# An RG-LRU block on both channel halves at once, and its steps run beside the RWKV's in the last third

## The chip, the cores and the metric

The kernel runs on one NeuronCore of a Trainium2 chip. The metric is the device time of one execution in microseconds (us). A core has five engines, each with its own instruction queue that is worked off in order: PE (TensorE, the matmuls), DVE (VectorE), ACT (ScalarE, activation functions), POOL (GpSimd) and SP (SyncE, which here issues DMAs). They wait for one another by semaphores. ACT evaluates functions from tables; an ACT_TABLE_LOAD row is the load of another set of functions.

## The reference, cut to what matters

One layer of a hybrid streaming encoder on 2048 tokens (with 16 learned tokens ahead, T = 2064) of width 1024, in fp32. One input projection feeds three head groups; their outputs go through one output projection, and a gated FFN with a short convolution follows.

```python
p  = rms_norm(h, norm_mix_pre) @ w_in                  # 1024 -> 512 | 1544 | 1024 columns
xa, ya = split(p[..., :512]);  pb = p[..., 512:2056];  pc = p[..., 2056:]
oa = rg_lru_group(xa, ya, ...)                         # 256 channels: the change is here
ob = forgetting_attention_group(pb, ...)               # 8 heads of 64, causal
oc = rwkv7_group(pc, ...)                              # 4 heads of 64, a recurrence over tokens
h  = h + rms_norm(concat([oa, ob, oc]) @ w_out, norm_mix_post)
...                                                    # FFN: up, conv of 3, gelu(g) * v, down

def rg_lru_group(xa, ya, ...):
    u = causal_dwconv(xa, conv_w) + conv_b             # 4 taps
    r = sigmoid(u @ ga_w + ga_b);  i = sigmoid(u @ gx_w + gx_b)      # per head of 64
    log_a = -8 * r * softplus(-lam);  a = exp(log_a)
    b = sqrt(-expm1(2 * log_a)) * (i * u)
    h_t = a_t * h_{t-1} + b_t                          # scan over tokens
    return h * gelu(ya)
```

## The kernel before, in words

Every large fp32 matmul is made of three passes over operands that are split into a high and a low half (`mm3`, L174 to L176). The stages follow one another: the input projection in three parts of the tokens (784, 768 and 512 columns), attention, the output projection, the FFN's up projection and its down projection. In each part of the input projection 24 units of output columns are computed (`psp` tiles on PE); ACT and DVE empty PSUM (`stp`, `sth`, `stl`), and the rows go to DRAM (`scr_p`). Between parts the next tokens are normalised, transposed and split (`w_in_norm`, tiles `xh`, `xl`).

Beside the projection run the two recurrences. `Beside.advance` is called once per unit of the projection and steps a queue of Python generators at a pace of 1.25 steps a call; a part's generator, `recurrences`, is added after 14 units. What is left at the projection's end is issued by `beside.finish()`, ahead of attention. The generator takes blocks of 256 tokens, nine in all, three per part: (0, 1, 2), (3, 4, 5), (6, 7, 8). The first block has 208 tokens and the last 64. For each block it steps the RWKV's preparation and its triangular solve (`R.block`, up to the mark `SOLVED`), then the ending of the RWKV block before (`R.ending`), and then the RG-LRU block (`lru_block`, L1432 to L1490).

The RG-LRU block works on 128 channels at a time, so everything in it is done twice, for the halves p = 0 and 1. For each half: the raw rows come by DMA into `rwlraw`; the convolution is one activation (L1455) and three instructions on DVE (L1457); two matmuls give the gates (L1462, L1463, into the one PSUM buffer `eps`); activations and DVE instructions form a and b, among them the root (L1478); the scan is one DVE instruction (L1480); the second raw tile and a tanh form gelu(y) (L1484 to L1488); the product (L1489) goes to DRAM by one DMA (`scr_mix`). The root needs another table than Exp and Tanh, so an ACT_TABLE_LOAD stands before the root (L1478), and another before whichever activation of the other set comes next (L1487, L1077, L1078, or attention's L698). `rwlraw` and the result tile `rwlu` have two buffers, the other tiles one.

The order on each engine isn't written by hand: a scheduler arranges the program's instructions by a simulated timeline, and the program's order is one input to it. Each engine then works its queue in the order found. The attention (`Attn.run`, L823) starts behind the last projection unit in program order, and its first matmuls (`mx`, `sc`, `po`) share the engines with the RWKV's last blocks. `mc` is its maximum on DVE (L571), `p` its exponential on ACT (L698), `q` its query tiles, whose extra rows are filled by memsets (L469, L487 to L489).

Of the kernel before, what the change touches and what calls it, by code (L numbers as in the profile page):

```python
# [1 line left out]

# [981 lines left out]
class Rwkv:  # L984
# [127 lines left out]
    def chunks(self, b, nch, sg, rav, bk, wc, bon):  # L1112
# [321 lines left out]
def lru_block(core, R, scr, k, b):  # L1434

    nc = core.nc
    t0 = max(0, Rwkv.start(b))
    n = min(T, Rwkv.start(b + 1)) - t0
    c0 = PAD + t0
    tt = nc.vector.tensor_tensor  # L1440
    stt = nc.vector.scalar_tensor_tensor

    def tl(s):
        return R.t([P, 256], s, bufs=2 if s == "lu" else 1)[:, :n]

    def raw(row, a):
        t = R.t([P, 260], "lraw", bufs=2)[:, : c0 + n - a]
        nc.sync.dma_start(t, scr["p"][row : row + P, a : c0 + n])
        return t

    for p in range(2):
        pc = slice(p, p + 1)
        x = raw(P * p, c0 - 3)
        u, r, g, al = (tl("l" + s) for s in ("u", "r", "g", "a"))
        nc.scalar.activation(u, x[:, 3:], AF.Identity, scale=k["conv_w"][:, 6 + p : 7 + p], bias=k["conv_b"][:, pc])  # L1455
        for i in range(3):
            stt(u, x[:, i : n + i], k["conv_w"][:, 2 * i + p : 2 * i + p + 1], u, op0=ALU.mult, op1=ALU.add)  # L1457


        ps = R.pe()  # L1460
        pa, px = ps[:, :n], ps[:, 256 : 256 + n]
        nc.tensor.matmul(pa, k["ga_w"][:, p], u, start=True, stop=True)  # L1462
        nc.tensor.matmul(px, k["gx_w"][:, p], u, start=True, stop=True)  # L1463
        nc.scalar.activation(r, pa, AF.Abs, bias=k["ga_b"][:, pc])
        nc.vector.tensor_scalar(al, pa, k["ga_b"][:, pc], 0.0, op0=ALU.add, op1=ALU.min)
        nc.scalar.activation(g, px, AF.Tanh, scale=0.5, bias=k["rate"][:, 2, pc])
        nc.scalar.activation(r, r, AF.Tanh, scale=0.5)
        nc.scalar.activation(al, al, AF.Exp)
        stt(r, r, 1.0, al, op0=ALU.add, op1=ALU.mult)
        stt(g, g, 1.0, u, op0=ALU.add, op1=ALU.mult)  # L1470
        yield
        nc.scalar.activation(al, r, AF.Exp, scale=k["rate"][:, 0, pc])
        nc.scalar.activation(r, r, AF.Tanh, scale=k["rate"][:, 1, pc])

        tt(u, al, al, op=ALU.mult)
        stt(r, u, 1.0, r, op0=ALU.add, op1=ALU.mult)
        nc.vector.tensor_scalar(r, r, 1e-34, None, op0=ALU.max)
        nc.scalar.activation(r, r, AF.Sqrt)  # L1478
        stt(g, g, 0.5, r, op0=ALU.mult, op1=ALU.mult)
        nc.vector.tensor_tensor_scan(u, al, g, k["h"][:, pc], op0=ALU.mult, op1=ALU.add)  # L1480
        nc.vector.tensor_copy(k["h"][:, pc], u[:, n - 1 : n])

        ya, y = raw(2 * P + P * p, c0), r
        nc.scalar.activation(y, ya, AF.Square)  # L1484
        nc.vector.tensor_scalar(y, y, 0.044715, 1.0, op0=ALU.mult, op1=ALU.add)
        tt(y, y, ya, op=ALU.mult)
        nc.scalar.activation(y, y, AF.Tanh, scale=0.7978845608028654)  # L1487
        stt(y, y, 1.0, ya, op0=ALU.add, op1=ALU.mult)  # L1488
        stt(u, u, 0.5, y, op0=ALU.mult, op1=ALU.mult)  # L1489
        nc.sync.dma_start(scr["mix"][P * p : P * p + P, t0 : t0 + n], u)  # L1490
        yield

# [599 lines left out]
def recurrences(core, R, lk, f_bias, scr, blocks, part):  # L2092
# [14 lines left out]
_INS = [  # L2107
# [294 lines left out]
```

## Time and profile before

| what | value |
|---|---|
| time, three runs | 2982.83, 2985.45, 2989.7 us (median 2985.45) |
| profiled execution | 2982.66 us, span 2981.0 us, mean granted PE clock 0.974 |
| PE busy | 2855.9 us, 96% of the span |
| DVE busy | 2024.3 us, 68% |
| ACT busy | 1504.8 us, 50% |
| POOL busy | 1308.5 us, 44% |
| DMA | 530.51 MB, mean 178 GB/s |

The page has the busy time of each engine, the busy share in 40 slices, the chain of work that ended last (followed back from the end, at each step to what released it), and groups of instructions by source line. "L1478" is line 1478 of the kernel before; after the change the same code stands one to five lines lower. A group's row reads: line, engine, operation, output<-inputs, shapes, xcount | busy us, mean ns of one | idle us of the engine just ahead of them, and who ended that idle time. In the windows view a row is a stretch of the span. By the trace the first part of the projection runs with recurrences from about 150 us, the crossing to the second part lies at 285 to 325, the second part and its crossing up to about 640, the third part until about 855, and the RWKV's last blocks beside attention until about 1065 or a little later. Attention lasts to about 1500 us.

### The profile page before, as it was taken

The numbers are of one execution on the slowest core, as the hardware profiler recorded it, in microseconds if no ns is written. First come the engines' busy times: TensorE is split into PE (matmuls) and PEld (weight loads), VectorE is DVE, ScalarE is ACT, GpSimd is POOL, SyncE is SP. The second block draws the span as 40 slices with busy tenths as digits, with TensorE's granted clock in tenths as the row PEclk, the third lists the DMA queues.
The fourth block names the chain that finished last, engine by engine and source line by source line (L and its number), as shares of the span: only waits on it lengthen the run. The fifth ranks groups of instructions, "written<-read, shape, count | busy, mean of one in ns | idle before, by whom it ended". The sixth has DMA issues, their size and how long they took to land.

```text
span 2981.0 us, 53287 instructions
## 1 busy us (share of the span) xinstructions
PE 2855.9 (96%) x18826; PEld 2447.1 (82%) x18826; DVE 2024.3 (68%) x3957; ACT 1504.8 (50%) x2937; POOL 1308.5 (44%) x1569
## 2 busy tenths in 40 slices
PE   6999999999988889999999999999999999999998
PEld 6998899888875554566568999999999999787887
DVE  5257754665687766665546988798778777656766
ACT  4246432454346554455634666656565665324333
POOL 1001121132124566566842666455655444646443
PEclk8999899999988899999999999999999999999999
DMA  6776479576653348445245665576767764436453
GB/s 217 234 233 220 143 251 322 179 242 219 219 131 78 85 118 225 105 104 125 66 125 190 200 192 173 171 225 210 211 208 216 220 196 134 156 114 222 145 174 120
DMA packets 470343, 530.51 MB, mean 178 GB/s; under 512 B 86862, under 2 KB 356888, under 8 KB 468524
## 3 DMA queue, kind: packets, MB, share of 16 engines
q1 hardware_dynamic: 469308, 526.18, 58.4%
q8 instruction: 148, 2.42, 0.3%
q0 software_dynamic: 768, 0.93, 0.1%
q14 instruction: 119, 0.97, 0.1%
HBM read 368.07 MB, written 158.90 MB: 177 GB/s over the span
## 4 chain that ended last, share of the span: by engine, by line
PE 73%; DVE 8%; DMA 7%; ACT 4%; POOL 4%; issue 2%; SPq 1%; DVEq 0%; POOLq 0%; ACTq 0%
PE psu L174 9%; PE psu L175 9%; PE psu L176 9%; PE psp L176 4%; PE psp L174 4%; PE psp L175 4%; PE psd L174 4%; PE psd L175 4%; PE psd L176 4%; PE po L716 3%; PE pswo L174 2%; PE pswo L175 2%; PE pswo L176 2%; PE mx L566 2%; PE sc L693 2%
## 5 line engine op out<-in xcount | busy, mean ns | idle before, releaser
L175 PE MATMUL psu<-xo,uw 128*128 128x344 f32 x1848 | 592.4, 321 | 0.0
L174 PE MATMUL psu<-xo,uw 128*128 128x344 f32 x1848 | 587.0, 322 | 3.1 <-DVE vb L1870 2.8
L176 PE MATMUL psu<-xo,uw 128*128 128x344 f32 x1848 | 582.6, 320 | 0.6 <-DVE uw L1679 0.6
L174 PE MATMUL psp<-xh,wh 128*128 128x384 f32 (+2 forms) x1152 | 378.3, 328 | 1.4 <-DMA wh<-scr_wk 1.4
L176 PE MATMUL psp<-xh,wl 128*128 128x384 f32 (+2 forms) x1152 | 376.3, 327 | 0.5 <-DMA wl<-scr_wk 0.5
L175 PE MATMUL psp<-xl,wh 128*128 128x384 f32 (+2 forms) x1152 | 375.0, 326 | 0.0
L1679 DVE TENSOR_TENSOR uw<-uq,uw 128x512 fp32r<-128x512 f32 x341 | 316.0, 931 | 63.7 <-ACT uw L1678 60.3
L174 PEld LDWEIGHTS psu<-xo,uw 128*128 128x128 f32 x1848 | 346.4, 188 | 4.2 <-DVE vb L1870 3.6
L175 PEld LDWEIGHTS psu<-xo,uw 128*128 128x128 f32 x1848 | 347.8, 188 | 0.0
L176 PEld LDWEIGHTS psu<-xo,uw 128*128 128x128 f32 x1848 | 346.4, 188 | 1.4 <-DVE uw L1679 1.4
L1678 ACT ACTIVATE uw<-uq 128x512 fp32r<-128x512 f32 x462 | 287.8, 627 | 103.6 <-PE psu L176 52.9
L698 ACT ACTIVATE p<-sc,bias 128x512 f32<-128x512 f32 (+4 forms) x352 | 197.5, 590 | 156.3 <-PE sc L694 126.1
L571 DVE TENSOR_REDUCE mc<-mx 128x1 f32<-128x512 f32 (+5 forms) x352 | 190.7, 566 | 117.5 <-PE mx L566 83.0
L1818 DVE SCALAR_TENSOR_TENSOR uy<-psu,ffn_cols,uy 128x342 f32<-128x342 f32 (+1 forms) x390 | 220.7, 567 | 60.9 <-ACT uy L1816 59.1
L737 POOL TENSOR_TENSOR acc<-acc,p 128x512 f32<-128x512 f32 (+3 forms) x208 | 222.3, 1072 | 62.4 <-DVE acc L737 28.3
L1826 POOL TENSOR_TENSOR uy<-uy,uy 128x342 f32<-128x342 f32 (+1 forms) x132 | 147.1, 1115 | 228.7 <-DVE uy L1818 59.5
L1679 POOL TENSOR_TENSOR uw<-uq,uw 128x512 fp32r<-128x512 f32 x121 | 185.4, 1532 | 134.1 <-ACT uw L1678 115.3
L176 PEld LDWEIGHTS psp<-xh,wl 128*128 128x128 f32 x1152 | 218.0, 189 | 8.4 <-issue 5.8
L174 PEld LDWEIGHTS psp<-xh,wh 128*128 128x128 f32 x1152 | 217.8, 189 | 8.4 <-issue 4.5
L175 PEld LDWEIGHTS psp<-xl,wh 128*128 128x128 f32 x1152 | 217.8, 189 | 7.2 <-issue 5.7
L1679 DVE TENSOR_TENSOR fo<-u,fo 128x896 fp32r<-128x896 f32 x88 | 101.1, 1149 | 132.3 <-ACT fo L1678 130.4
L1678 ACT ACTIVATE fo<-u 128x896 fp32r<-128x896 f32 x88 | 81.2, 923 | 209.0 <-PE psd L176 108.1
(489 smaller groups left out, 6326.2 us busy)
## 6 DMA issues: line engine op xcount, KB each, us to landing
uq<-scr_us SPq DMA_DIRECT2D x220, 256.0 KB
uq<-in_ffn_up_dram SPq DMA_DIRECT2D x209, 256.0 KB
wl<-scr_wk SPq DMA_DIRECT2D x48, 512.0 KB
wh<-scr_wk SPq DMA_DIRECT2D x48, 512.0 KB
u<-scr_ff SPq DMA_DIRECT2D x88, 256.0 KB
scr_ff<-uy SPq DMA_DIRECT2D x110, 171.0 KB
raw<-in_w_in_dram SPq DMA_DIRECT2D x24, 512.0 KB
scr_wk<-wh SPq DMA_DIRECT2D x24, 512.0 KB
```

The lines of the kernel that those rows point to most:

```text
L174: nc.tensor.matmul(out, ah, bh, start=first, stop=False, skip_group_check=more)
L175: nc.tensor.matmul(out, ah, bl, start=False, stop=False, skip_group_check=more)
L176: nc.tensor.matmul(out, al, bh, start=False, stop=last, skip_group_check=more)
L566: nc.tensor.matmul(ps[:rows, : e - a], q3[:, qo : qo + rows], k2[:, a:e], start=True, stop=not last)
L571: self.reduced = nc.vector.tensor_reduce(mc[:rows, i, ci : ci + 1], ps[:rows, : e - a], axis=AX.X, op=ALU.max)
L698: last = nc.scalar.activation(p[:rows, :w], ps[:rows, :w], AF.Exp, bias=bias[:rows, j : j + 1])
L716: mm = nc.tensor.matmul(po[at : at + 64, c0:n], v1[:rows, j], p[:rows, : n - c0], start=start and i < 2, stop=end and i + 2 >= len(group), ...
L737: eng.tensor_tensor(a, ps_[0][0][:rows, c0:n] if start and i == 1 else a, p[:rows, : n - c0], op=ALU.add)
L1678: core.nc.scalar.activation(hi, src, AF.Copy)
L1679: (eng or core.nc.vector).tensor_tensor(lo, src, hi, op=ALU.subtract)
L1818: core.conved = stt(y[:, :n], src[:, i : n + i], cw[:, 44 * i + cc : 44 * i + cc + 1], y[:, :n], op0=ALU.mult, op1=ALU.add)
L1826: core.pooled = nc.gpsimd.tensor_tensor(v[:, :n], g[:, :n], v[:, :n], op=ALU.mult)
```

## The change

`lru_block` works on both halves at once: its tiles are [128, 2, 256], with one buffer each (before, two for `lu` and `lraw`). One DMA fetches the raw rows of both halves, one stores the result. The convolution, the matmuls, the activations with a bias or scale per channel and the scan are still issued per half; ten DVE instructions and five activations are issued once for both halves. So there is one root a block. The block is cut into four steps of the generator, as before, but elsewhere.

In the projection's last third the RG-LRU steps of blocks 6, 7 and 8 are chained into one generator, `early`, which is advanced by one step with every step of the RWKV's solve and of its ending; before, each of these blocks came behind the whole solve and ending of its number. In the first two thirds the place of the block stays. A scratch tile of the RWKV's last block is 12 instead of 16 wide.

```diff
+from itertools import chain
...
-        og = w3 if nch == 4 else self.t([P, 16, P], "xu")
+        og = w3 if nch == 4 else self.t([P, 12, P], "xu")
...
     def tl(s):
-        return R.t([P, 256], s, bufs=2 if s == "lu" else 1)[:, :n]
+        return R.t([P, 2, 256], s)[:, :, :n]
 
     def raw(row, a):
-        t = R.t([P, 260], "lraw", bufs=2)[:, : c0 + n - a]
-        nc.sync.dma_start(t, scr["p"][row : row + P, a : c0 + n])
+        t = R.t([P, 2, 260], "lraw")[:, :, : c0 + n - a]
+        nc.sync.dma_start(t, scr["p"][row : row + 2 * P, a : c0 + n].rearrange("(p r) t -> r p t", p=2))
         return t
...
+    act = nc.scalar.activation
+    x = raw(0, c0 - 3)
+    u, r, g, al = (tl("l" + s) for s in ("u", "r", "g", "a"))
     for p in range(2):
...
+        act(u[:, p], x[:, p, 3:], AF.Identity, scale=k["conv_w"][:, 6 + p : 7 + p], bias=k["conv_b"][:, pc])
...
+        act(r[:, p], pa, AF.Abs, bias=k["ga_b"][:, pc])
+        nc.vector.tensor_scalar(al[:, p], pa, k["ga_b"][:, pc], 0.0, op0=ALU.add, op1=ALU.min)
+        act(g[:, p], px, AF.Tanh, scale=0.5, bias=k["rate"][:, 2, pc])
+    yield
+    act(r, r, AF.Tanh, scale=0.5)
+    act(al, al, AF.Exp)
+    stt(r, r, 1.0, al, op0=ALU.add, op1=ALU.mult)
+    stt(g, g, 1.0, u, op0=ALU.add, op1=ALU.mult)
+    for p in range(2):
+        pc = slice(p, p + 1)
+        act(al[:, p], r[:, p], AF.Exp, scale=k["rate"][:, 0, pc])
+        act(r[:, p], r[:, p], AF.Tanh, scale=k["rate"][:, 1, pc])
+    yield
+    tt(u, al, al, op=ALU.mult)
+    stt(r, u, 1.0, r, op0=ALU.add, op1=ALU.mult)
+    nc.vector.tensor_scalar(r, r, 1e-34, None, op0=ALU.max)
+    act(r, r, AF.Sqrt)
+    stt(g, g, 0.5, r, op0=ALU.mult, op1=ALU.mult)
+    for p in range(2):
+        pc = slice(p, p + 1)
+        nc.vector.tensor_tensor_scan(u[:, p], al[:, p], g[:, p], k["h"][:, pc], op0=ALU.mult, op1=ALU.add)
+        nc.vector.tensor_copy(k["h"][:, pc], u[:, p, n - 1 : n])
+    yield
+    ya, y = raw(2 * P, c0), r
+    act(y, ya, AF.Square)
...
+    stt(u, u, 0.5, y, op0=ALU.mult, op1=ALU.mult)
+    nc.sync.dma_start(scr["mix"][0 : 2 * P, t0 : t0 + n].rearrange("(p r) t -> r p t", p=2), u)
+    yield
...
-    for b in ((0, 1, 2), (3, 4, 5), (6, 7, 8))[part]:
+    bs = ((0, 1, 2), (3, 4, 5), (6, 7, 8))[part]
+    early = chain.from_iterable(lru_block(core, R, scr, lk, b) for b in bs if part == 2)
+    for b in bs:
         gen = R.block(b)
         while next(gen) != R.SOLVED:
+            next(early, None)
             yield
-        yield from R.ending
+        for _ in R.ending:
+            next(early, None)
+            yield
         R.ending = gen
-        yield from lru_block(core, R, scr, lk, b)
+        if part < 2:
+            yield from lru_block(core, R, scr, lk, b)
```

What the scheduler makes of it is seen in the order of each engine. On PE, before, the gates of one half of block 7 (`eps` tiles, written from `rwlu`) stand among attention's first maxima and scores:

```order
L693 MATMUL sc_11586<-q_1444_11397,k_1424_11324 128x512
L694 MATMUL sc_11586<-q_1433_11344,k_1425_11325 128x512
L579 MATMUL mx_11512<-ident,sh_11510 1x128 x2
L1135 MATMUL rps_9956<-rwrav_9902,rwbk_9909 64x128 x8
L1462 MATMUL eps_10537<-rwlu_10529,lru_ga_w 128x256
L1463 MATMUL eps_10537<-rwlu_10529,lru_gx_w 128x256
L579 MATMUL mx_11512<-ident,sh_11510 1x128 x2
L566 MATMUL mx_11537<-k_1425_11325,q_1427_11329 128x400
```

Now the last gates of the kernel, those of block 8's second half, stand within the projection's last unit:

```order
L175 MATMUL psp_10291<-xh_6593,wh_10112 128x256
L176 MATMUL psp_10291<-xl_6594,wh_10112 128x256
L1463 MATMUL eps_9220<-rwlu_9202,lru_ga_w 128x64
L1464 MATMUL eps_9220<-rwlu_9202,lru_gx_w 128x64
L177 MATMUL psp_10291<-xh_6593,wl_10113 128x256
L175 MATMUL psp_10291<-xh_6593,wh_10112 128x256
```

So all RG-LRU matmuls moved ahead of the projection's end. Of the 3456 matmul rows of the projection, the gates of blocks 6, 7 and 8 now stand behind 3058, 3277 and 3413 of them; before, block 6 stood behind 3265 and the other two behind the last.

On ACT, at the crossing from the projection's first part to its second, these pieces stood before (`xh` is the split of the next tokens, `rww`, `rwsc`, `rwe` are the RWKV's):

```order
L1478 ACT_TABLE_LOAD
L1478 ACTIVATE rwlr_2971<-rwlr_2971 128x256
...
L1487 ACT_TABLE_LOAD
L1487 ACTIVATE rwlr_2971<-rwlr_2971 128x256
...
L1478 ACT_TABLE_LOAD
L1478 ACTIVATE rwlr_3071<-rwlr_3071 128x256
L1261 ACTIVATE rww_202_1647<-rps_2642 64x8x64 x2
L1078 ACT_TABLE_LOAD
L1078 ACTIVATE rwe_3379<-rwe_3379 128x512
```

And now:

```order
L152 ACTIVATE xh_3091<-pst_3224 128x4x128
L1481 ACT_TABLE_LOAD
L1481 ACTIVATE rwlr_2947<-rwlr_2947 128x512
L152 ACTIVATE xh_3091<-pst_3231 128x4x128
L1083 ACTIVATE rwsq_3343<-rwe_3331,rwkv_om 128x256
L1489 ACTIVATE rwlr_2947<-rwlraw_3080 128x512
L1253 ACTIVATE rwxf_2363<-rps_2599 32x8x32 x2
L1492 ACT_TABLE_LOAD
L1492 ACTIVATE rwlr_2947<-rwlr_2947 128x512
```

Two roots of 256 columns with a table load before and behind each became one root of 512 with one pair of loads. Over the kernel, ACT_TABLE_LOAD rows fall from 54 to 36.

On DVE, before, the RWKV's last reciprocal root (rows of 4x256) stood ahead of the projection's last `stl`:

```order
L77 SCALAR_TENSOR_TENSOR rwitmp_9834<-rwix_9833 4x256
L78 TENSOR_TENSOR rwitmp_9834<-rwitmp_9834,rwia_9832 4x256
L1273 COPY rwxu_9339<-rps_9352 128x256
L79 SCALAR_TENSOR_TENSOR rwix_9833<-rwitmp_9834,rwix_9833 4x256
L241 SCALAR_TENSOR_TENSOR stl_10299<-psp_10273,sth_10298 128x256
```

Now it stands among and behind attention's memsets and its first maxima:

```order
L1494 SCALAR_TENSOR_TENSOR rwlu_9202<-rwlu_9202,rwlr_9203 128x2x64
L490 MEMSET q_1378_11124 1x512
L76 TENSOR_SCALAR rwix_9664<-rwia_9663 4x256
...
L572 TENSOR_REDUCE mc_11150<-mx_11152 128x1
L78 SCALAR_TENSOR_TENSOR rwitmp_9665<-rwix_9664 4x256
L572 TENSOR_REDUCE mc_11150<-mx_11156 128x1
L1106 SCALAR_TENSOR_TENSOR rwsq_9657<-rwsq_9657,rwkv_cols,rwr_9724 128x256 x2
```

So the last of the RG-LRU has taken the place of RWKV work there: 21 RWKV rows of DVE that stood ahead of attention's first memset now stand behind it, and 56 of the RG-LRU's 58 rows behind it moved ahead of it. POOL's order and the count of PE's instructions stay the same; SP issues 27 DMAs fewer.

More of the change, by code (lines that the diff above doesn't have):

```diff
@@ L1451, in lru_block @@
+    x = raw(0, c0 - 3)
+    u, r, g, al = (tl("l" + s) for s in ("u", "r", "g", "a"))
     for p in range(2):
         pc = slice(p, p + 1)
-        x = raw(P * p, c0 - 3)
-        u, r, g, al = (tl("l" + s) for s in ("u", "r", "g", "a"))
-        nc.scalar.activation(u, x[:, 3:], AF.Identity, scale=k["conv_w"][:, 6 + p : 7 + p], bias=k["conv_b"][:, pc])
+        act(u[:, p], x[:, p, 3:], AF.Identity, scale=k["conv_w"][:, 6 + p : 7 + p], bias=k["conv_b"][:, pc])
         for i in range(3):
-            stt(u, x[:, i : n + i], k["conv_w"][:, 2 * i + p : 2 * i + p + 1], u, op0=ALU.mult, op1=ALU.add)
+            w = k["conv_w"][:, 2 * i + p : 2 * i + p + 1]
+            stt(u[:, p], x[:, p, i : n + i], w, u[:, p], op0=ALU.mult, op1=ALU.add)
@@ L1460, in lru_block @@
         ps = R.pe()
         pa, px = ps[:, :n], ps[:, 256 : 256 + n]
[L1462 to L1488, printed above, removed]
@@ L1489, in lru_block @@
-        stt(u, u, 0.5, y, op0=ALU.mult, op1=ALU.mult)
-        nc.sync.dma_start(scr["mix"][P * p : P * p + P, t0 : t0 + n], u)
-        yield
+        nc.tensor.matmul(pa, k["ga_w"][:, p], u[:, p], start=True, stop=True)
+        nc.tensor.matmul(px, k["gx_w"][:, p], u[:, p], start=True, stop=True)
+        act(r[:, p], pa, AF.Abs, bias=k["ga_b"][:, pc])
+        nc.vector.tensor_scalar(al[:, p], pa, k["ga_b"][:, pc], 0.0, op0=ALU.add, op1=ALU.min)
+        act(g[:, p], px, AF.Tanh, scale=0.5, bias=k["rate"][:, 2, pc])
```

4 lines of the change are left out of this document (added).

## The prediction

> **What bounds the kernel now.** I started with the page's chain that ended last, to see whether any engine but TensorE matters at all.
>
> ```profile
> PE 73%; DVE 8%; DMA 7%; ACT 4%; POOL 4%; issue 2%; SPq 1%; DVEq 0%; POOLq 0%; ACTq 0%
> ```
>
> Over the whole span TensorE sets the end, and the RG-LRU block hardly touches TensorE. So the change can only pay where TensorE waits. The windows by stage say where that is (columns: window, length, then busy time of PE, PEld, DVE, ACT, POOL with their instructions, granted clock, DMA share, GB/s).
>
> ```profile
> core 0: us, PE busy (x) PEld busy (x) DVE busy (x) ACT busy (x) POOL busy (x), PEclk, DMA share, GB/s
> 285.00:325.00 40.00, 31.82 (x461) 27.41 (x460) 32.72 (x93) 29.17 (x61) 11.19 (x22) 0.74 0.36 117
> 325.00:640.00 315.00, 310.11 (x2619) 281.96 (x2615) 180.90 (x446) 119.94 (x237) 61.74 (x91) 0.99 0.74 243
> 640.00:855.00 215.00, 203.77 (x2482) 185.07 (x2480) 141.05 (x380) 106.24 (x228) 49.75 (x86) 1.00 0.63 198
> 855.00:1065.00 210.00, 177.10 (x1761) 120.74 (x1757) 160.44 (x452) 115.18 (x255) 100.18 (x161) 0.83 0.41 98
> 1065.00:1200.00 135.00, 121.85 (x641) 67.31 (x639) 88.09 (x197) 68.71 (x134) 83.90 (x105) 0.97 0.70 181
> ```
>
> The projection ends near 855 us. The stretch behind it, 855 to 1065, is the weak one: TensorE idles 210 − 177.1 = 32.9 us, and its clock is 0.83, so a further 0.17 × 210 = 35.7 us goes to a halved clock. This is where the RWKV recurrence and the last RG-LRU blocks share DVE and ACT with the first attention heads. The second weak place is the crossing from the projection's first part to its second, 285 to 325: 8.2 us idle and a clock of 0.74. The projection's last third, 640 to 855, idles 215 − 203.8 = 11.2 us at full clock; this is where the change puts work.
>
> Then the chain within 855 to 1065, by line, and a few of its pieces in order of time (start, length, what).
>
> ```profile
> by line: PE po L716 8.2%; PE mx L566 5.7%; issue 5.2%; DVE mc L571 4.4%; PE sc L693 4.3%; PE sc L694 3.1%; DMA dx<-rwix 3.0%; ACT p L698 3.0%; DVE o L785 2.3%; ACT L1478 2.3%; PE rps L1291 2.2%; PE mx L579 2.1%; ACT L698 1.8%; DMA rwraw<-sc
> 911.42 1.28 ACT L1478
> 913.04 0.36 ACT rww L1168
> 914.20 1.28 ACT L698
> 915.50 0.49 ACT p L698
> ```
>
> No single line holds this stretch; the chain hops between engines every half microsecond. But two entries without a tile name, "ACT L1478" and "ACT L698", are table loads: the first brings in the root's table for the RG-LRU, the second brings the exponential's back for attention. They hold 2.3% and 1.8% of 210 us, 4.8 + 3.8 = 8.6 us. The groups of ACT in that window confirm what they are.
>
> ```profile
> L1478 ACT ACT_TABLE_LOAD x4 | 5.1, 1283 | 0.1
> L698 ACT ACT_TABLE_LOAD x3 | 3.8, 1283 | 0.1
> L1487 ACT ACT_TABLE_LOAD x1 | 1.3, 1283 | 0.0
> ```
>
> Four half blocks (both halves of blocks 7 and 8) run there, with two loads each.
>
> **The change part by part.** *The tail, 855 to 1065.* All matmuls of the RG-LRU move ahead of the projection's last ones, and with them every table load: 8.6 us of chain go. The rest of the block's work there, by the tiles that carry it (columns of rwlr: DVE, ACT; of rwlu: PE, PEld, DVE, ACT):
>
> ```profile
> 640.00:855.00 215.00, 19.00 (x45) 16.95 (x38) 1.00 0.63 198
> 855.00:1065.00 210.00, 12.05 (x32) 10.30 (x28) 0.83 0.41 98
> 640.00:855.00 215.00, 5.50 (x20) 3.33 (x20) 24.21 (x51) 3.60 (x6) 1.00 0.63 198
> 855.00:1065.00 210.00, 3.41 (x16) 2.47 (x16) 11.14 (x30) 0.88 (x2) 0.83 0.41 98
> ```
>
> Tail: DVE at most 12.05 + 11.14 = 23.2 us (some instructions touch both tiles, so this is an upper end). In exchange the RWKV falls behind a little: by the order lists 21 of its DVE instructions that stood ahead of attention's first memset now stand behind it, ten of them rows of the reciprocal root at 4x256. I price all 21 by this row:
>
> ```profile
> L77 DVE SCALAR_TENSOR_TENSOR rwitmp<-rwix 4x256 f32<-4x256 f32 x24 | 10.4, 432 | 0.4
> ```
>
> 21 × 0.43 = 9.0 us. Net relief of DVE 23.2 − 9.0 = 14.2 us. DVE is busy 160.4 of 210 us but TensorE waits only 32.9, so most of what DVE sheds is covered by other work; I count a quarter, 3.5 us. Term: 8.6 + 3.5 = **−12 us**. Bounds: 0, if attention's own matmuls and reductions (po, mx, mc lead the chain) close up behind the loads; −23, if all of 8.6 + 14.2 counts. I stay in the middle, since the loads stand on the chain by row and the DVE part does not.
>
> *The crossing, 285 to 325.* Here are the pieces of its chain that the RG-LRU causes:
>
> ```profile
> 289.91 1.28 ACT L1487
> 307.69 1.28 ACT L1478
> 310.65 1.28 ACT L1078
> 318.00 2.01 DMA scr_mix<-rwlu
> 320.09 0.61 ACT rwlu L1455
> ```
>
> Before, two halves pass here, with two pairs of loads between the splits of the next part's tokens; after, one pair serves both, so 2 × 1.283 = 2.6 us go. The merged instructions save their starting cost. Rows of whole stages, 256 against 512 columns:
>
> ```profile
> L1475 DVE TENSOR_TENSOR rwlu<-rwla 128x256 f32<-128x256 f32 x14 | 6.3, 447 | 0.6 <-ACT rwla L1472 0.6
> L1099 DVE TENSOR_TENSOR rwbk<-rwsq,rwe 128x512 f32<-128x512 f32 x8 | 5.7, 713 | 0.0
> L1467 ACT ACTIVATE rwlr<-rwlr 128x256 f32<-128x256 f32 x14 | 5.8, 414 | 0.3
> L1078 ACT ACTIVATE rwe<-rwe 128x512 f32<-128x512 f32 x8 | 5.0, 624 | 1.5 <-DVE rwe L1075 1.5
> ```
>
> Two of 256 cost 2 × 447 = 894 ns on DVE, one of 512 713: 0.18 us saved, ten times a block, 1.8 us. ACT: 2 × 414 − 624 = 0.20 us, five times, 1.0 us. Half of these 2.8 us on the chain is 1.4. Term: 2.6 + 1.4 = **−4 us**. Bounds: −8 (both pairs leave the crossing, 5.1, and all 2.8 count) and +4: the copies of raw rows and of the result tile went from two to one, so a block's conv can wait for the block before to be stored, as "DMA scr_mix<-rwlu" 2.01 us already shows, twice.
>
> *The last third, 640 to 855.* Blocks 7 and 8 come in: 23.2 us of DVE less the merging. DVE has 215 − 141 = 74 us to spare and ACT 109. Table loads don't grow: six halves pass here now, each with a root, and five blocks with one root each pass afterwards. Idle of TensorE there is 11.2 us with six halves, so at most 1.9 us is due to each. Four halves more at half of that: **+4 us**. Bounds: 0 (covered) and +8 (1.9 each). What sits behind a block's waits on ACT and DVE is the emptying of the projection's PSUM, so this cover is not free; the first rival starts from it.
>
> *The rest.* In other stretches the blocks stay where they were with shorter work. TensorE is busy 310.1 of 315 us in 325 to 640, so I take 0, with ±4 for the reshuffled order later. The number of loads over all blocks falls from 18 pairs to 9:
>
> ```profile
> L1478 ACT ACT_TABLE_LOAD x18 | 23.1, 1283 | 0.3
> L1487 ACT ACT_TABLE_LOAD x11 | 14.1, 1283 | 0.2
> ```
>
> Nine roots' loads and nine returns fewer are 23 us of ACT in all, but ACT is half idle, so beyond the two places above they are covered.
>
> A page bears on this. The Trainium skill, "ScalarE: Activation LUTs", section "What ACT_TABLE_LOAD costs", gives about 1283 ns for the load plus about 1380 ns of drain for each switch. The load agrees with the rows here. The drain does not show: the load at 914.20 ends at 915.48 and the next activation starts at 915.50. By the page the tail would gain 8 × 1.38 = 11 us more, an estimate, and the sum would be −23; by the trace nothing is added, and I go by the trace.
>
> Sum: −12 − 4 + 4 = −12 us. The profiled execution took 2982.66, so 2970.7. It lies 2.8 us under the median of the three runs (2985.45), so against them I say **2973.5**. For the forecast's own range I let each term go half way to its bounds: −5.5, −2, −2, −2 below and +6, +4, +2, +2 above; added in squares, as they are unrelated, that is −6.5 and +7.7, so 2967 to 2981.
>
> **The rivals.** *Slower: single buffers in in-order queues hold the projection.* Three blocks now follow each other within block 6's solve and block 5's ending, each with two raw loads into one buffer and one result tile. The wait exists already:
>
> ```profile
> ACT rwlu L1455 <- DMA scr_mix<-rwlu: 5.9, 2, 3.4
> ACT stp L57 <- PE psp L176: 13.5, 3, 8.6
> L1455 ACT ACTIVATE rwlu<-rwlraw,lru_cols 128x256 f32<-128x256 f32 x14 | 8.4, 598 | 24.3 <-DMA scr_mix<-rwlu 11.4 <-DMA rwlraw<-scr_p 11.4 <-DVE rwix L1186 1.5
> ```
>
> The longest was 3.4 us. ACT empties PSUM (stp) in the same queue, so 3 × 2 × 3.4 = 20.4 us of it held up could starve TensorE. And a stall halves its clock as in the crossing: 0.26 × 40 = 10.4 us lost beside 8.2 us of idle. Up to 30.8 in place of the +4 makes −16 + 30.8 = +15: **3000**. It decides from about 22 us of new stall in that stretch. Against it: today TensorE waits 13.5 us on nobody here, ACT waits for TensorE (second row), so ACT runs ahead and has slack; and five PSUM buffers stand between.
>
> *No difference.* The tail's end is set by the RWKV's chain and attention's heads, whose places against each other on TensorE hardly move, and the freed microseconds turn into waits. For it: po, mx, sc lead the chain there. Then the tail gives 0 to −3 and crossing and third cancel: −3, **2982.5**.
>
> *Larger gain through the clock.* The tail loses 35.7 us to a clock of 0.83. If fewer hops on DVE and ACT close enough gaps to bring it to 0.89, 0.06 × 210 = 12.6 us come on top: −25, **2960.5**. For it: the gaps are short ones made by such hops. Against: the order of the RWKV and attention stays, and other hops remain.
>
> **How the numbers follow.** Forecast 0.53, no difference 0.22, larger gain 0.12, slower 0.13. A measurement of this kernel can tell about 0.2% or 6 us from no change. Faster by more than that: most of the forecast (0.48) and the larger gain (0.12), with a little of the third case, 0.62. Slower: the slower rival but for its small end, and stray, 0.13. The remaining 0.25 is no difference. The range takes in the no-difference case whole and half of each outer one: 2960 to 2988.
>
> **What would show it.** Tail: no table load for the root and none of L698 between the projection's end and the last recurrence, TensorE's idle there down from 32.9 to about 22, its clock at 0.83 or above. Crossing: one pair of loads on the chain. Last third: TensorE's idle under 16 us, clock still 1.00. Loads for the root 9 times rather than 18, and groups of 512 columns near 0.71 us on DVE and 0.62 on ACT. The forecast is wrong if the last third grows by more than 10 us, with ACT or DVE waiting for raw rows or stored results just ahead of a late emptying of PSUM; or if the loads vanish from the tail and its length stays, which would mean that they only filled a wait for something else.

## The result and the profile after

The changed kernel is slower: 1.0034 of the time before (95% interval 1.0023 to 1.0044), medians 2997.14 against 2987.52 us over 14 executions of each, so about +10 us where 12 us less were forecast. Executions of one kernel spread by some ±8 us around their median. The profiled execution after took 3002.86 us (span 3001.2) and lies in the upper part of its spread, that of before (2982.66) in the lower part of its own. The two profiles therefore differ by 20 us, and a stretch of one profile is good to a few us only.

To compare stretches I cut both traces at the same matmuls rather than at the same times: at matmuls 864, 1584 and 2592 of the projection and its last one, then at matmuls 440 and 1056 of attention and at its last. The windows of before (window, length, busy time of PE, PEld, DVE, ACT, POOL, granted clock, DMA share, GB/s):

```profile
206.13:433.91 227.78, 217.69 (x1900) 194.25 (x1899) 150.69 (x391) 116.36 (x227) 41.54 (x72) 0.95 0.60 194
433.91:681.59 247.68, 241.81 (x2163) 218.87 (x2163) 154.86 (x388) 101.17 (x211) 55.63 (x82) 0.99 0.75 249
681.59:855.64 174.05, 165.30 (x1947) 150.70 (x1945) 109.02 (x298) 81.94 (x175) 35.01 (x62) 1.00 0.61 191
855.64:1050.19 194.55, 161.74 (x1636) 110.77 (x1634) 148.60 (x419) 107.32 (x238) 90.46 (x143) 0.82 0.42 99
1050.19:1209.02 158.83, 144.29 (x792) 80.28 (x791) 105.94 (x246) 81.79 (x161) 98.94 (x136) 0.95 0.64 166
1209.02:1526.38 317.36, 308.89 (x1406) 188.96 (x1402) 179.30 (x358) 166.38 (x302) 223.01 (x303) 0.99 0.38 93
```

And the same stretches of the changed kernel:

```profile
207.19:449.29 242.10, 220.01 (x1890) 196.23 (x1889) 147.23 (x360) 105.48 (x206) 46.33 (x72) 0.92 0.57 182
449.29:698.01 248.72, 240.30 (x2138) 217.66 (x2137) 146.67 (x355) 93.28 (x194) 57.37 (x82) 0.99 0.75 247
698.01:883.59 185.58, 173.84 (x1959) 159.49 (x1957) 119.95 (x308) 84.74 (x183) 37.56 (x61) 0.95 0.60 183
883.59:1067.06 183.47, 157.94 (x1659) 107.89 (x1658) 138.79 (x376) 91.47 (x204) 86.85 (x142) 0.84 0.42 98
1067.06:1226.84 159.78, 142.18 (x792) 79.89 (x792) 112.23 (x249) 83.74 (x166) 103.04 (x132) 0.96 0.66 170
1226.84:1548.69 321.85, 313.61 (x1404) 189.36 (x1401) 184.46 (x361) 166.81 (x302) 227.78 (x308) 0.99 0.38 92
```

Row by row: the stretch with the first crossing +14.3 us, the middle +1.0, the last third +11.5, the tail (projection's end to attention matmul 440) −11.1, the rest of attention +1.0 and +4.5. So the tail gave what was forecast, and the crossing and the last third took it back twice over. These differences add up to 21 us, twice the difference of the medians, as the two profiles are themselves 20 us apart.

At the crossing TensorE's idle rose from 10.1 to 22.1 us. Before, the longest wait of TensorE between 285 and 325 us was this (engine, tile and line, what it waited for and where that was made, total, times, longest):

```profile
PE rps L1215 <- ACT rwsc L1168: 3.5, 1, 3.5
```

The waits of the changed kernel there name two places:

```profile
PE rps L1216 <- ACT rwe L1079: 8.4, 1, 8.4
DVE rwe L1073 <- DMA rwia<-da: 6.3, 1, 6.3
PE rps L1216 <- DVE rwxu L1246: 5.7, 2, 5.6
```

The waits of SP's queue between 280 and 300 us name what stands behind the first:

```profile
SPq L1714 <- POOL us L1712: 4.7, 1, 4.7
```

L1714 stores the first sums of the FFN's weights, a piece of work beside the projection that has nothing to do with the RG-LRU. SP stands 4.7 us at it until POOL has made the sums, and behind it in the queue is the RWKV's solve: eight small copies `da`, then its loads `rwia`. The order of SP's queue there, changed kernel on the left of the arrow, kernel before on the right:

```
L1714 DMA scr_us<-us                     ->   L1153 DMA da<-rwsc x8
L1154 DMA da<-rwsc x8                         L242  DMA scr_qh<-sth
L128  DMA xt<-in_x_dram                       L243  DMA scr_ql<-stl
L128  DMA xt<-in_x_dram                       L1158 DMA rwia<-da x2
L1159 DMA rwia<-da x2                         ...
                                              L1709 DMA scr_us<-us
```

The loads of the solve were issued at 296.06 us instead of 287.39 (issue times of the SP rows `rwia<-da`). The second gap is on DVE. Its timeline ahead of the copy L1246 for which TensorE waits 5.6 us:

```profile
312.81 0.43 DVE L1480 TENSOR_SCALAR rwlr<-rwlr 128x512 f32<-128x512 f32 x1
...
314.36 0.68 DVE L1482 SCALAR_TENSOR_TENSOR rwlg<-rwlg,rwlr 128x512 f32<-128x512 f32 x1
...
316.60 1.56 DVE L1485 TENSOR_TENSOR_SCAN rwlu<-rwla,lru_h,rwlg 128x256 f32<-128x256 f32 x2
318.20 0.88 DVE L1246 COPY rwxu<-rps 32x256 f32<-32x256 f32 x2
```

Of the 5.4 us between the solve's piece before it and the copy, 2.7 are RG-LRU pieces, now in lengths of 512 or two scans in a row; the other half are pieces of other work, the splits `xl` of the next tokens above all. Before, 1.1 us stood between the same two, with two RG-LRU pieces of 256:

```profile
301.42 0.42 DVE L1470 SCALAR_TENSOR_TENSOR rwlg<-rwlg,rwlu 128x256 f32<-128x256 f32 x1
...
301.88 0.42 DVE L1469 SCALAR_TENSOR_TENSOR rwlr<-rwlr,rwla 128x256 f32<-128x256 f32 x1
302.33 0.88 DVE L1245 COPY rwxu<-rps 32x256 f32<-32x256 f32 x2
```

In the last third the largest waits of ACT and of TensorE in the changed kernel between 850 and 875 us are

```profile
ACT rwlu L1457 <- DMA scr_mix<-rwlu: 3.9, 1, 3.9
PE rps L1216 <- DMA rwlraw<-scr_p: 2.0, 1, 2.0
```

and windows across the place, with the columns as above:

```profile
840.00:859.00 19.00, 18.14 (x154) 17.06 (x150) 11.82 (x25) 12.97 (x30) 1.79 (x4) 1.00 0.43 123
859.00:871.00 12.00, 8.76 (x197) 8.17 (x198) 8.36 (x30) 5.33 (x12) 4.50 (x9) 0.76 0.30 96
871.00:876.40 5.40, 5.40 (x53) 5.11 (x53) 3.12 (x10) 0.70 (x2) 1.02 (x2) 0.50 0.06 12
876.40:890.00 13.60, 10.46 (x132) 8.89 (x130) 5.64 (x18) 9.75 (x23) 4.72 (x5) 0.88 0.25 68
```

Block 8's convolution (L1457) waits 3.9 us on ACT until block 7's result has left the one tile `rwlu`. TensorE idles 3.2 us in 859 to 871, and works at half clock from 865.24 to 878.89 us. By the windows 0.24 × 12 + 0.50 × 5.4 + 0.12 × 13.6 = 7.2 us are lost; half of 13.65 is 6.8, and the rest belongs to a later stretch at half clock that begins at 889.1. Not all of the idle is due to the store: a gap of 2.0 us, at the RWKV's solve, ends at 865.32 while ACT still waits, and 0.9 us is the wait of block 8's first gate (L1463, at 869.24) for that convolution. The whole third's busy time of TensorE is 8.5 us up at a clock of 0.95 instead of 1.00, its idle 3.0 us.

What the change does to the block itself came out as priced. The groups by line, shapes apart, from 150 to 1120 us:

```profile
L1478 DVE TENSOR_TENSOR rwlu<-rwla 128x512 f32<-128x512 f32 x7 | 4.8, 682 | 1.2 <-ACT rwla L1475 1.2
L1489 ACT ACTIVATE rwlr<-rwlraw 128x512 f32<-128x512 f32 x7 | 4.4, 625 | 2.8 <-DVE rwlg L1482 2.8
L1481 ACT ACT_TABLE_LOAD x9 | 11.5, 1283 | 10.1 <-DVE rwlr L1480 10.0
```

and the root's and the RWKV's loads among the groups of the tail, 883 to 1067 us:

```profile
L1481 ACT ACT_TABLE_LOAD x1 | 1.3, 1283 | 0.0
L1078 ACT ACT_TABLE_LOAD x1 | 1.3, 1283 | 0.0
```

Nine loads for the root instead of 18, and two loads left in the tail of eight.

### The profile page after: what moved, and what is told of

Same layout as the page of the kernel before. It is cut to its first block, busy times and chain, and to the rows that moved or that the text cites. A ratio compares the mean times of both kernels' runs of the same rounds, so it can differ in the third digit from the quotient of the medians.

```text
span 3001.2 us, 53118 instructions
## 1 busy us (share of the span) xinstructions
PE 2863.0 (95%) x18826; PEld 2452.5 (82%) x18826; DVE 2025.8 (68%) x3867; ACT 1474.8 (49%) x2874; POOL 1322.2 (44%) x1569
## 4 chain that ended last, share of the span: by engine, by line
PE 66%; DVE 8%; DMA 4%; POOL 3%; ACT 2%; issue 2%; SPq 1%; DVEq 0%; POOLq 0%; ACTq 0%
PE psu L175 9%; PE psu L176 9%; PE psu L177 9%; PE psd L175 4%; PE psd L176 4%; PE psd L177 4%; PE po L717 4%; PE mx L567 2%; PE psp L177 2%; PE psp L175 2%; PE pswo L175 2%; PE psp L176 2%; PE pswo L176 2%; PE pswo L177 2%; PE sc L694 2%
## 5 line engine op out<-in xcount | busy, mean ns | idle before, releaser
L572 DVE TENSOR_REDUCE mc<-mx 128x1 f32<-128x512 f32 (+6 forms) x352 | 189.9, 565 | 117.7 <-PE mx L567 84.8
```

The lines of the kernel that those rows point to most:

```text
L572: self.reduced = nc.vector.tensor_reduce(mc[:rows, i, ci : ci + 1], ps[:rows, : e - a], axis=AX.X, op=ALU.max)
```

## The experiments

Twelve kernels ran, two of them a second time. The ratios are to the kernel before, with 95% intervals; the stretches are read from one profile each, cut at the same matmuls, in us.

| kernel | ratio | crossing 864 to 1584 | last third 2592 to end | tail to attention 440 |
|---|---|---|---|---|
| before | 1 | 227.8 | 174.1 | 194.6 |
| changed kernel | 1.0034 (1.0023 to 1.0044) | 242.1 | 185.6 | 183.5 |
| after_again | one execution | 239.7 | 188.9 | 184.9 |
| block_only | 0.9993 (0.9984 to 1.0002) | 241.9 | 177.2 | 177.0 |
| early_only | 0.9996 (0.9986 to 1.0006) | 227.2 | 176.7 | 190.6 |
| after_store_later | 1.0017 (1.0005 to 1.0029) | 237.4 | 185.1 | 179.8 |
| block_store_later | 0.9985 (0.9973 to 0.9998) | 235.8 | 175.8 | 179.8 |
| one_halves | 1.0007 (0.9996 to 1.0019) | 234.2 | 176.6 | 192.5 |
| two_halves | 0.9937 (0.9923 to 0.9950) | 224.7 | 176.5 | 183.1 |
| after_own8 | 1.0013 (1.0002 to 1.0023) | 241.6 | 179.7 | 174.1 |
| halves_then_both | 1.0018 (1.0006 to 1.0030) | 222.8 | 181.9 | 183.6 |
| halves_then_early | 0.9909 (0.9893 to 0.9926) | 223.0 | 175.7 | 166.1 |
| halves_early_again | 0.9891 (0.9878 to 0.9904) | 222.7 | 170.9 | 162.1 |
| halves_early_own8 | 1.0002 (0.9992 to 1.0013) | 222.9 | 179.4 | 174.4 |

**The two parts apart.** block_only has the new block at the old place:

```diff
-    early = chain.from_iterable(lru_block(core, R, scr, lk, b) for b in bs if part == 2)
...
         R.ending = gen
-        if part < 2:
-            yield from lru_block(core, R, scr, lk, b)
+        yield from lru_block(core, R, scr, lk, b)
```

> The both-halves block with one root, but in the last third at its old place, behind the RWKV's solve and ending. Queue theory (the order of SP's DMA queue at the crossing 285 to 325 us makes the loss: there the store of the first FFN sums stands ahead of the RWKV solve's small copies and holds them 4.7 us; this kernel has the same SP queue up to the third part): TensorE's idle between projection matmuls 864 and 1584 is again about 22 us rather than 10, and the kernel is about 10 us slower than before, +0.3%. Early theory (the loss is made by running three blocks ahead of the projection's end): no slower than before, within 5 us.

early_only has the old block, with the new order of steps:

```diff
+    early = chain.from_iterable(lru_block(core, R, scr, lk, b) for b in bs if part == 2)
...
+            next(early, None)
```

> The block by halves with two roots as before, but its steps in the last third run along with the RWKV's solve and ending. Queue theory: the crossing is that of before (idle about 10 us between projection matmuls 864 and 1584), so only the last third and the tail differ; what the tail gives (about 10 us) and what the third takes (8 to 12 us) cancel: within 6 us of before. Early theory: 8 to 12 us slower than before, with the loss in 640 to 885 us.

Each part alone is level with before. The crossing's loss belongs to the block (241.9 against 227.2), as the queue theory said, but its total of +10 us was wrong: block_only gets 17.6 us back in the tail, more than the whole change. And the early theory's loss doesn't come with the early steps alone: 176.7 us in the last third with two roots. The two together take 185.6 in the changed kernel; but one_halves, two_halves and halves_then_early below have both in this third too and take 176.6, 176.5 and 175.7. So the two together aren't enough for the loss, and the order in which they came to stand has a part in it.

The tail of block_only, its window:

```profile
874.83:1051.79 176.96, 153.88 (x1634) 104.92 (x1633) 143.71 (x402) 98.96 (x223) 88.47 (x141) 0.86 0.46 108
```

and the table loads among its groups there:

```profile
L1481 ACT ACT_TABLE_LOAD x2 | 2.6, 1283 | 2.7 <-DVE rwlr L1480 2.7
L699 ACT ACT_TABLE_LOAD x2 | 2.6, 1283 | 0.0
```

The tail of early_only, its window:

```profile
855.69:1046.28 190.59, 163.37 (x1668) 110.62 (x1667) 139.84 (x409) 101.19 (x227) 89.66 (x142) 0.82 0.42 97
```

and the table loads among its groups:

```profile
L1479 ACT ACT_TABLE_LOAD x3 | 3.8, 1283 | 0.1
L1488 ACT ACT_TABLE_LOAD x2 | 2.6, 1283 | 0.0
L1078 ACT ACT_TABLE_LOAD x1 | 1.3, 1283 | 0.0
```

The first of these six begins 0.9 us ahead of the tail, so five of the eight are left in it. The tail that keeps blocks 7 and 8 and four loads is shorter by 17.6 us; the one from which more than half of their work has gone (DVE's on RG-LRU tiles falls from 21.7 to 9.5 us), by 4.0. So neither the moving nor the number of loads sets the tail's length in this pair; the new block goes with the shorter one.

**The store on SP's queue.** after_store_later puts the one store behind the solve's loads again; up to attention that is the only row that moves on any engine's queue:

```diff
+        if b == 1:
+            core.asked = ask          # the last of the loads L1159
...
-        nc.sync.dma_start(out[:, :, z : z + n], t[:])
+        with core.tc.issue_after(core.asked.ins) if j == js[0] and z == 0 else nullcontext():
+            nc.sync.dma_start(out[:, :, z : z + n], t[:])
```

> The changed kernel with one difference: the first store of the FFN sums is put behind the RWKV solve's loads on SP's queue, as it stood before the change; no other row of SP, ACT, DVE or PE moves up to attention. Queue theory: TensorE's idle between projection matmuls 864 and 1584 falls from 22 to 12 to 15 us, and the kernel is 6 to 10 us faster than the changed one, so about level with before (0 to +4 us). Block theory (the merged block with its single buffers holds the crossing): idle stays at about 22 us and the time about 10 us above before. Early theory: the same 10 us above before.

block_store_later makes the same edit in block_only.

> The both-halves block at its old place (as block_only), with the first store of the FFN sums behind the RWKV solve's loads on SP's queue. Queue theory: another 4 to 6 us off block_only by the first gap at the crossing (8 us to about 3), so 5 to 8 us faster than before. If the queue's wait is covered by later slack: level with block_only (-2 us against before).

The window of the crossing in after_store_later:

```profile
205.50:442.90 237.40, 219.13 (x1890) 195.54 (x1889) 147.22 (x360) 105.59 (x206) 44.38 (x72) 0.94 0.58 186
```

Its largest wait of TensorE there:

```profile
PE rps L1218 <- DVE rwxu L1248: 6.2, 1, 6.2
```

TensorE's idle in the stretch is 18.3 us instead of 22.1, and the second gap stays, under its line numbers in this kernel. The first gap falls from 8.4 to 2.7 us, and in the other pair from 7.9 to 2.0. The crossing is 4.7 and 6.1 us shorter in the two pairs (in the first pair 2.3 against the second profile of the changed kernel, below), and the totals go the same way, by 0.0017 and 0.0008, the latter within its noise. So the store's place is shown to cost about 5 us, a third of the crossing's loss; the queue theory's 6 to 10 was too much, and the idle of 18.3 us lies outside its 12 to 15, as it lies under the block theory's 22.

**The block at the crossing.** one_halves makes block 1, the one that stands at the crossing, by halves with two roots, as before; the store stays ahead of the solve:

```diff
+    if b == 1:
+        ...        # the old block, half after half, in the halves of the new tiles
+        return
```

> The changed kernel with block 1 alone, the one that stands at the first crossing, by halves with two roots; on SP's queue the store of the FFN sums still stands ahead of the solve's copies. Queue theory (the store's place alone makes the crossing's loss): from projection matmul 864 to 1584 again 240 to 242 us, idle about 22. Two causes (the store some 5 us, the longer merged pieces ahead of the solve's copies on DVE some 8): 231 to 235 us, idle 13 to 17, and 4 to 8 us off the changed kernel. Block theory (the merged block alone): 223 to 228 us, as with halves throughout.

two_halves does so for blocks 0 and 1; the scheduler then puts the store behind the solve's loads by itself.

> The changed kernel with blocks 0 and 1 by halves, which moves the store of the FFN sums back behind the solve's loads too. By the two causes: the crossing (projection matmuls 864 to 1584) at 222 to 228 us, 12 to 17 us shorter than in the changed kernel, and so 0 to 6 us faster than before if the rest stays as in the changed kernel (last third 185 to 189, tail 183 to 185). If the order behind the crossing shifts again: the crossing at 222 to 228 all the same, the total anywhere from -20 to +5 us.

The window of the crossing in one_halves:

```profile
205.44:439.67 234.23, 219.88 (x1900) 194.96 (x1899) 147.65 (x372) 109.39 (x213) 42.32 (x72) 0.95 0.58 189
```

That of two_halves:

```profile
207.28:431.93 224.65, 214.78 (x1890) 191.90 (x1889) 150.75 (x380) 112.89 (x220) 41.29 (x72) 0.96 0.62 197
```

234.2 us with an idle of 14.3 is what two causes were to give, and the second gap behind L1246 is gone. But the first gap is smaller too, 3.1 us instead of 8.4, though the store is still ahead: SP stands 2.6 us at it instead of 4.7. So the merged block also lengthened the store's wait, and the two causes aren't independent. The tail of one_halves, however, takes 192.5 us, though blocks 2 to 8 have the new block and run early as in the changed kernel: an edit in block 1 has moved the rows of the tail by way of the scheduler, and 9 us with them. With both taken away the crossing is 17.4 us shorter than in the changed kernel, 3.1 shorter than before. The two causes don't simply add (4.7 to 6.1 and 7.9 make 13 to 14), and block 0 is by halves there as well. And two_halves as a whole is faster than before, 0.9937.

**A second profile of the changed kernel.**

> The changed kernel once more, for a second profile. If the two large gaps of TensorE at the first crossing come from the order of the queues, they stand here again: about 8 and 6 us, 22 us idle between projection matmuls 864 and 1584. If they were an accident of one execution, the idle there is near 10 us.

The gaps stand again, 22.6 us of idle in 239.7, and so does the last third. The queues' order makes them, not one execution.

**The single buffer.** after_own8 gives block 8 a raw tile and a result tile of its own:

```diff
+        if b == 8 and s == "lu":
+            return R.t([P, 2, n], "lu8")[:]
...
-        t = R.t([P, 2, 260], "lraw")[:, :, : c0 + n - a]
+        t = R.t([P, 2, 260 if b < 8 else n + 4], "lraw" if b < 8 else "lraw8")[:, :, : c0 + n - a]
```

> The changed kernel with a raw tile and a result tile of its own for block 8, so that its convolution doesn't wait for block 7's result to be stored. Buffer theory (in the last third the one buffer holds ACT 3.9 us behind block 7's store, the solve's copies queue behind it, and TensorE's gaps of 4 to 5 us between 859 and 870 us halve its clock for 13.7 us): those gaps fall below 2 us, the stretch from projection matmul 2592 to its last one takes 176 to 179 us rather than 185 to 189, and the kernel is 5 to 10 us faster than the changed one (0 to +5 us against before). Work theory (the stretch is longer because more RG-LRU work stands in it at all): 184 us or more, and no faster than the changed kernel by more than 3 us.

Windows of the last third and of the two places in it:

```profile
697.24:876.89 179.65, 171.96 (x1959) 157.49 (x1957) 119.49 (x309) 84.84 (x183) 35.75 (x61) 0.96 0.61 189
859.00:871.00 12.00, 9.84 (x183) 9.42 (x182) 10.75 (x30) 5.72 (x12) 4.71 (x9) 0.86 0.23 78
871.00:876.40 5.40, 5.40 (x88) 4.58 (x87) 3.03 (x10) 3.82 (x11) 0.47 (x1) 1.00 0.28 88
```

The wait for the store is gone from the waits there, the last third is 5.9 to 9.2 us shorter than in the two profiles of the changed kernel, and 0.0021 of the time goes, about as the buffer theory said (its 176 to 179 us for the third are missed by a little). A gap of 2.2 us at the RWKV's solve stays, but behind it the clock is halved for 3.41 us instead of 13.65. The tail is 9.4 us shorter as well, so the total can't be put down to the wait alone. Nor does the wait alone decide. In two_halves, with the single tiles, it stands in the last third, longer than in the changed kernel:

```profile
ACT rwlu L1508 <- DMA scr_mix<-rwlu: 5.1, 1, 5.1
```

and that third takes 176.5 us. What differs is the place of block 8's gates on TensorE's queue. In the three long thirds (the changed kernel's two profiles and after_store_later, 185 to 189 us) the first of them stands behind 3413 of the 3456 projection matmuls, and TensorE waits 0.9 to 2.0 us for it; in one_halves and two_halves it stands behind the last of them and in halves_then_early behind 3443, and TensorE doesn't wait for it. By these traces the wait costs time where such a gate stands ahead of projection matmuls; no run moved the gate alone.

**Halves first, both later.** halves_then_both makes blocks 0 to 5 by halves and only 6 to 8 with one root, at the old place; halves_then_early lets these three run early, as in the change; halves_early_own8 adds block 8's own tiles.

```diff
+    if b < 6:
+        ...        # the old block, half after half, in the halves of the new tiles
+        return
```

> Blocks 0 to 5 by halves with two roots, as before the change (in the merged tiles), blocks 6 to 8 on both halves with one root, and these at their old place behind the RWKV's solve and ending. Crossing theory (the merged block costs about 14 us at the first crossing, in part by the store of the FFN sums ahead of the solve on SP's queue, in part by longer pieces of RG-LRU work ahead of the solve's copies on DVE; one root a block gives about 15 us back in the tail): idle between projection matmuls 864 and 1584 about 10 us as before, the tail 10 to 15 us shorter, so 6 to 12 us faster than before (-0.2 to -0.4%). Tail theory (the tail only catches up because the projection ended late, and gives nothing when it ends in time): within 4 us of before.

> As halves_then_both, but blocks 6 to 8 run early as in the change. Crossing theory: the crossing is that of before, the last third 5 to 9 us longer, the tail about 10 shorter: 0 to 5 us faster than before, and 4 to 8 us slower than halves_then_both. Tail theory: 5 us slower than before.

> As halves_then_early (blocks 0 to 5 by halves, 6 to 8 merged and early, 0.9909 of before), and block 8 with tiles of its own. Buffer theory: its last third has one gap of 4.3 us; if it is the same wait, 2 to 6 us faster than halves_then_early, 0.988 to 0.990 of before. If its gain comes from a lucky order that any new place upsets: 5 us or more slower than halves_then_early.

> halves_then_early once more: if its 0.9909 of before is a property of its order, 0.989 to 0.993 again, with a tail (projection's end to attention matmul 440) near 166 us; if it was those executions alone, 0.996 or more.

All four have the short crossing of 223 us, and halves_then_both has the shorter tail too that the crossing theory gave it (183.6 us). But the stretch between the crossing and the last third is longer in all four, 254.8 to 259.1 us against 247.7 before; here that of halves_then_both, with 2208 matmuls instead of 2163, so in part it is work that moved in:

```profile
429.95:689.09 259.14, 249.83 (x2208) 225.03 (x2207) 158.14 (x391) 102.00 (x211) 55.47 (x87) 0.97 0.72 237
```

The totals came the other way round than I expected. The version that I forecast as the best is slower than before, 1.0018; the one with the early steps is the best of all, 0.9909 and again 0.9891, by the medians 26 to 30 us faster than before and 35 or more faster than the change; and to give it another buffer takes all of that away, 1.0002. That is what the second theory for halves_early_own8 said: the gain is that of a lucky order, which any new place upsets. It repeats with this kernel, but it isn't a worth of the edit. The tail of halves_then_early, its window:

```profile
864.55:1030.60 166.05, 151.36 (x1667) 102.63 (x1665) 136.83 (x388) 93.30 (x211) 85.00 (x141) 0.90 0.46 106
```

and the largest wait of TensorE in it:

```profile
PE rps L1312 <- DVE rstate L1316: 3.5, 2, 2.6
```

In the changed kernel the same waits in the tail are

```profile
PE mx L580 <- DVE sh L577: 4.8, 2, 4.1
PE rps L1292 <- ACT rww L1276: 4.3, 1, 4.3
```

two waits of over 4 us that halves_then_early hasn't, 25.5 us of idle against 14.7 and a clock of 0.84 against 0.90. It is the same RG-LRU work in both, with another place among the RWKV's and attention's rows. Which of the places does it wasn't separated by a run and stays open.

## Why the prediction was wrong

**The tail was right in size, and that was luck as far as the runs show: its reason isn't borne out.** −12 us were forecast, −11.1 and −9.6 measured, idle 25.5 (forecast about 22), clock 0.84. But the step "8.6 us of chain go" with the loads doesn't hold: block_only keeps half the loads there and gains 17.6, early_only loses three of the eight and gains 4.0. Nor did every load leave, as I had written: a root's and a return's (L1481 and L1078) still stand in the tail. And one_halves, with the new block and the early steps in its tail as in the change, gains only 2.0 there. Over all the kernels with some of the new block the tail lies between 162 and 193 us, in no order of their loads (halves_early_own8 has none there and takes 174.4): its length hangs on where the RG-LRU's rows come to stand among the others, and that my 12 us came out is not shown to be for my reason. My term took the two entries of the chain for its cause because they had a name of their own in the row.

**The crossing failed, and that is the step that turned the sign.** I wrote "one pair serves both, so 2 × 1.283 = 2.6 us go" and 1.4 for the merged instructions, −4 with bounds of −8 and +4. Both savings exist (nine loads; 0.68 and 0.63 us a merged instruction), and the stretch is 11.9 to 14.3 us longer. Two things were missing. SP's queue, which after_store_later shows: about 5 us, since a store that waits for POOL was now ahead of the solve's copies. I had compared the orders of ACT, DVE and PE at this place and of SP only the count of DMAs. And the merged block 1 itself, which one_halves shows: 5.4 to 7.9 us against the two profiles of the changed kernel, part of it through the store's wait. How it costs them is only read from DVE's timeline: 5.4 us stood ahead of the solve's small copy instead of 1.1, and in them were longer RG-LRU pieces, more of them, and as much other work. No run changed the length alone, so whether length or order counts stays open. I counted what merging saves an engine, not what the new order would make another one wait for.

**The last third was mis-sized.** +4 with an upper bound of 8 was forecast; +11.5 and +14.8 came. The mechanism was in part the one of my slower rival, to which I gave 0.13: a single tile, ACT held in order, TensorE idle and then at half clock; after_own8 takes 5.9 to 9.2 us of it away. Its price there, 20.4 of stall and 10.4 of clock, was too high for one block; the trace shows 3 us of idle and 7 to 8.5 of clock. The forecast's own term left out the clock, though the crossing's row had shown what a few us of idle cost. Even so the rival's condition, 22 us of new stall in that stretch, was never met: the loss came from the crossing and the last third, of which it named one. That the third takes 171 to 177 us in one_halves, two_halves and halves_then_early, with nearly the same work in it, suggests that the +4 was near for the work itself and that the rest came with the order.

**The rest** was 0 ± 4 and was +1.0, +1.0 and +4.5. The last, in attention's second half, stands in nearly all the kernels here (320 to 322.5 us against 317.4), so it isn't particular to the change.

**Table loads.** The Trainium skill, "ScalarE: Activation LUTs", section "What ACT_TABLE_LOAD costs", counts about 1380 ns of drain on top of the load for each switch of the table set. In the changed kernel ACT's activation ahead ends at 854.65, the load runs from 854.67 to 855.95, and the root's activation starts at 855.96; the drain doesn't show here either. By that rule 18 loads fewer would be worth 24.8 us more of ACT's time, an estimate; block_only, with as many loads fewer, is level with before, so no such gain shows in a total, though that run doesn't separate it.

What stays open is which places in the tail make it 17 to 21 us shorter in halves_then_early and its repeat than in the changed kernel, and 9 us longer in one_halves, and what makes the middle stretch longer in the four kernels of halves.

## What to carry to other kernels

Where an order is found by a scheduler, compare the order of every queue at the places that matter, the DMA queue first: a store that waits for a slow engine holds all the copies behind it, here 5 us from a row that the change didn't touch. Merging small instructions saves some of their time (here 0.2 us a pair) and can hold up whatever another engine needs in between; so look at what stands ahead of a chain's small pieces in the queue before and after, here 1.1 and 5.4 us. Before a change is kept or dropped, run its parts apart and in parts of the program: here the same edit was worth +0.3%, or −0.6% and −1% with its first two or first six blocks left as they were; and another buffer on top of the best of these took its gain away, so a total alone doesn't say what an edit is worth.

## What was not expected of the hardware

What a gap costs in clock isn't told by its length. In the last third of the changed kernel 3.2 us of idle within 12 us went with 13.65 us at half clock, 6.8 us lost; in after_own8 a gap of 2.2 us, and in two_halves one of 3.3, with 3.41 us; in halves_then_early a gap of 4.3 with 6.83. So the halved clock cost about twice the idle in the changed kernel and less than the idle in the three others. The stretches at half clock of the changed kernel, of after_own8 and of halves_then_early:

```profile
865.24:878.89 13.65, 12.72 (x171) 12.11 (x172) 7.71 (x25) 2.60 (x8) 2.81 (x6) 0.50 0.25 81
864.25:867.66 3.41, 3.41 (x77) 3.35 (x62) 3.22 (x9) 0.94 (x2) 1.58 (x3) 0.50 0.13 44
850.13:856.96 6.83, 6.71 (x128) 6.45 (x129) 6.15 (x18) 1.94 (x5) 2.87 (x5) 0.50 0.28 89
```

The Trainium skill, "TensorE: Matmul & The Clock Gate", Part 1, says that the gate knows only the full clock and half of it and counts activity in windows of about 3.4 us. The rows agree: the granted clock is 0.50 throughout each of these, and the stretches at half clock are one, two and four times 3.41 us long.
